# A sum of weights made by an accumulating transfer within SBUF, in place of an addition on VectorE

## The chip, the cores and the metric

The kernel runs on one core of one Trainium2 chip. The metric is device time in microseconds (us) of one execution; a lower time is better. Before the change it took 2020.15 us, the median of 3 runs (2019.51 to 2020.68).

## The reference

A decoder trunk of two layers, in float32, on 512 tokens with 16 learned tokens ahead (T = 528), width 1024, hidden width 2816. Cut to what matters here:

```python
def swiglu(x, w_in, w_out):
    gate, up = jnp.split(x @ w_in, 2, axis=-1)
    return (jax.nn.silu(gate) * up) @ w_out

for i in range(2):                                   # h: (528, 1024)
    h = h + 0.5 * swiglu(rmsnorm(h, norm_ffn1[i]), ffn1_w_in[i], ffn1_w_out[i])
    h = h + mixer_i(rmsnorm(h, norm_mix[i]))         # retention in layer 0, gated linear attention in layer 1
    h = h + 0.5 * swiglu(rmsnorm(h, norm_ffn2[i]), ffn2_w_in[i], ffn2_w_out[i])
return rmsnorm(h, final_norm)[:, 16:]
```

The change touches the last product of swiglu, `(...) @ w_out`, in each of the four feed-forward networks.

## The kernel before

**Names of the networks.** f1/0 and f2/0 are the networks ahead of and behind the mixer of layer 0, f1/1 and f2/1 those of layer 1. The first three are *feeding*: as their last columns of x are finished, the kernel already scales and splits them for the next block (`feed`). f2/1 is the last.

**Precision.** A float32 operand is split into a high part and a low part, and each product is three matmuls (`mm3`, L488 to L490): high by high, high by low, low by high. A weight tile of 128 rows by 512 (or 384) columns comes to SBUF as `raw`. ScalarE makes its high part by a cast (`whi`, L188) and VectorE its low part by a subtraction (`wlo`, L189). This pair of instructions stands once for each weight tile, some 1200 times in a run, and TensorE multiplies by the results four steps later at most (`AHEAD = 4`).

**Units.** Most products are done in *units*: two blocks of output rows and two halves of the tokens, by a scheme with seven products in place of eight. Its seven weight operands are a11, a12, a22 as loaded, s1 = a21 + a11, s3 = a21 + a22, s2 = s1 + a11 and s4 = a12 + s2 (signs are hidden in the data). Their order in a unit is a11, s1, s2, a12, s4, s3, a22 (`UNIT`). The first unit of a feeding network's last group has the order a11, s1, a12, s2, s4, s3, a22 (`PARTED`): its first three products are each done in two parts, so that work can begin before the last hidden rows are there. A unit's results are X (one bank) and Q, Z (two banks) in PSUM. The last product, a22, is held over and done inside the next unit. Each bank is emptied by ScalarE copies (L727, L729, L734: `szf<-X` and the like) or by VectorE additions before TensorE writes it again.

**How the sums are made.** For each unit, SP (SyncE's DMA queue) loads a11 and a22 into the two halves of a `pair` tile (L149), and GpSimd (POOL) then issues one transfer from HBM that adds a21 to both halves (L155; in some units two transfers, L153). The pair's halves then hold s3 and s1. a11, a12 and a22 are also loaded by SP as `raw` tiles (L158). After the split of a11, VectorE adds s1 to the raw tile of a11 (L195): that tile now holds s2. After the split of a12, VectorE adds s2 to the raw tile of a12 (L197): that tile now holds s4. There are 7 raw tiles and 3 pair tiles. GpSimd's queue holds little else than these transfers in the network stages; a transfer for a later unit waits there until its pair tile is free and its first halves are loaded.

**Out groups.** The 22 blocks of hidden rows are consumed in groups: 8, 6 and 8 in a feeding network, 6, 6, 6 and 4 in the last one. Group index 2 is the last group in a feeding network (8 blocks, four products of 128 columns of k: weight tiles of 128x512) and the third of four in f2/1 (6 blocks: 128x384). A group has four units, d = 0, 2, 4, 6, each for two of the eight blocks of x. Its units are called `unit_o`; the in-products are units too (`unit_g`, `unit_u`), with two units per pair of hidden blocks.

**Where results go.** The names carry the unit: Xf10u is the X bank of a u unit of f1/0, Xf10o that of an o unit. L1035 (`su<-Xf10u,su`) empties X of the last u unit on VectorE. L1069 and L1070 add an o unit's first row to x, L1076 and L1077 the second (`x<-szf,x`, then `x<-Xf10o,x`, which frees X); L1081 adds the a22 product. L576 and L592 scale, square and split x for the next block.

**What sets the order.** The program is written as one stream; a scheduler puts each engine's instructions into a row by priorities, and each engine runs its row strictly in order. An instruction that waits holds all that stands behind it on its engine. `_split` issues one operand's cast, subtraction and sums, and is called up to four steps ahead of the product that uses it.

Of the kernel before, what the change touches and what calls it, by code (L numbers as in the profile page):

```python
# [14 lines left out]
ALU = mybir.AluOpType  # L15
# [53 lines left out]
class Weights:  # L69
# [92 lines left out]
    def _split(self, upto):  # L162
        V = self.nc.vector
        while self.split < min(upto, len(self.plan)):
            i = self.split
            home = next(((pool, there) for pool, n, there in self.homes if len(there) < n), None)
            if not home:
                break
            home[1].add(i)
            _, c, q, n, order = self.plan[i]  # L170
            self._load()
            if order:

                late = order[0] == "s1"
                s2 = self.tiles[c][:, 1] if late else self.tiles[c, "a11"]
                raw = {"s1": self.tiles[c][:, 1], "s3": self.tiles[c][:, 0], "s2": s2,
                       "s4": self.tiles[c, "a12"]}.get(q)
            if not order or raw is None:
                raw = self.tiles[c, q]
            hi = home[0].tile([P, PW], F32R, tag="hi", name=f"whi{i}")  # L180
            lo = home[0].tile([P, PW], F32R, tag="lo", name=f"wlo{i}")
            with ExitStack() as order_:
                if self.behind and i < self.FRONT:
                    for ins in self.behind:
                        order_.enter_context(self.tc.issue_after(ins.ins))
                if self.after:
                    order_.enter_context(self.tc.issue_after(self.after.ins))
                act = self.nc.scalar.copy(hi[:, :n], raw)  # L188
                dve = V.tensor_sub(lo[:, :n], raw, hi[:, :n].bitcast(F32))  # L189
                self.newest = act, dve  # L190
            self.parts[i] = (hi, lo)
            self.split += 1
            if order:
                if q == ("s1" if late else "a11"):
                    V.tensor_add(s2, self.tiles[c][:, 1], self.tiles[c, "a11"])  # L195
                elif q == "a12":
                    V.tensor_add(raw, raw, s2)  # L197
                self.over["pair"] += q == "s3"
                self.over["raw"] += q in self.OVER[2 if order == self.PARTED else late]
            else:  # L200
                self.over["raw"] += 1
            self._load()
# [2146 lines left out]
```

## Time and profile before

One execution was profiled: its own time was 2020.17 us, its span 2018.4 us.

| | value |
|---|---|
| median of the runs | 2020.15 us (2019.51 to 2020.68) |
| profiled execution | 2020.17 us, span 2018.4 us, granted TensorE clock 0.999 |
| TensorE (PE) busy | 1998.6 us, 99% of the span, 16576 matmuls |
| VectorE (DVE) busy | 1793.7 us, 89%, 3302 instructions |
| ScalarE (ACT) busy | 1190.6 us, 59%, 2427 instructions |
| GpSimd (POOL) busy | 209.8 us, 10%, 181 instructions |
| casts of weights (L188, raw and pair) | 715.3 us on ACT, 1197 instructions |
| subtractions of weights (L189, raw and pair) | 792.1 us on DVE, 1197 instructions |
| sums on DVE, L195 and L197 | 97.2 us and 97.5 us, 146 of each in the usual form |
| moved by DMA | 318.87 MB, mean 158 GB/s |

How it is read: a share is busy time over the span. The page has, after the busy times, the span in 40 slices, the DMA queues (a queue's share is of 16 DMA engines over the span), the chain of work that ended last, and the groups of instructions by line, engine, operation and tiles. A row of single instructions gives the start, the duration, the engine, the line, the operation, the output and inputs, and in square brackets the idle time before it with what ended it. A line "DMA to landing" below a transfer gives the time from its issue to the moment when the last of its data has arrived. A row of waits gives the waiting engine, tile and line, what it waited for, and us in all, times, and the longest.

### The profile page before, as it was taken

Reading aid. Unit: us, or ns where it says so; the run is one execution under the profiler, and the core shown is the slowest. Engines: PE = TensorE matmul, PEld = TensorE weight load, DVE = VectorE, ACT = ScalarE, POOL = GpSimd, SP = SyncE. Lnnn points to the kernel's source line nnn. Section 1 sums busy time; section 2 is a strip of 40 time slices with the busy share of each in tenths; the row PEclk is TensorE's granted clock in tenths of the full one; section 3 lists DMA queues with packets and bytes.
Section 4 is the critical chain, followed back from the end, with each engine's and each line's share of the span. In section 5 each row is a group of like instructions: output and inputs, shape, how many; then the busy total and the mean of one; then the engine's idle time right before and its main releaser. Section 6 shows DMA issues by size and latency. Waiting matters only on the chain.

```text
span 2018.4 us, 43487 instructions
## 1 busy us (share of the span) xinstructions
PE 1998.6 (99%) x16576; PEld 1964.3 (97%) x16576; DVE 1793.7 (89%) x3302; ACT 1190.6 (59%) x2427; POOL 209.8 (10%) x181
## 2 busy tenths in 40 slices
PE   9999999999999999999999999999999999999998
PEld 9999999999999999999999999999999989999998
DVE  8999999978787889989999998999897868999896
ACT  5756566555555465656666665666745544666664
POOL 1011111010101000111111011111001000211110
PEclk9999999999999999999999999999999999999999
DMA  7586877364545432776875477777525441687772
GB/s 228 138 208 168 205 194 188 101 163 121 157 132 147 132 116 74 181 202 161 213 186 163 128 189 187 180 199 181 183 69 126 105 137 65 159 208 182 185 191 69
DMA packets 176113, 318.87 MB, mean 158 GB/s; under 512 B 17568, under 2 KB 40736, under 8 KB 175904
## 3 DMA queue, kind: packets, MB, share of 16 engines
q1 hardware_dynamic: 133856, 237.04, 35.8%
q0 software_dynamic: 40896, 75.51, 23.4%
q10 hardware_dynamic: 1152, 3.55, 0.6%
q8 instruction: 130, 2.13, 0.4%
q14 instruction: 79, 0.65, 0.1%
HBM read 311.76 MB, written 4.26 MB: 157 GB/s over the span
## 4 chain that ended last, share of the span: by engine, by line
PE 83%; DVE 12%; ACT 2%; issue 2%; DMA 1%; POOL 0%; POOLq 0%; DVEq 0%; ACTq 0%
DVE wlo L189 4%; PE po_r L488 1%; PE po_r L489 1%; PE po_r L490 1%; PE lv L1866 1%; ACT whi L188 1%; DVE hf L521 1%; PE Xf21o L488 1%; PE Xf21o L490 1%; PE Xf21o L489 1%; PE Xf20u L488 1%; PE Xf11u L488 1%; PE Xf20u L490 1%; PE Xf11u L490 1%; PE Xf11u L489 1%
## 5 line engine op out<-in xcount | busy, mean ns | idle before, releaser
L188 ACT CAST whi<-raw 128x512 fp32r<-128x512 f32 (+1 forms) x893 | 531.9, 606 | 424.6 <-DVE raw L197 145.9
L189 DVE TENSOR_TENSOR wlo<-raw,whi 128x512 fp32r<-128x512 f32 (+1 forms) x893 | 590.3, 669 | 104.6 <-ACT whi L188 91.4
L188 ACT CAST whi<-pair 128x512 fp32r<-128x512 f32 (+1 forms) x304 | 183.4, 604 | 75.1 <-DVE pair L195 12.4
L189 DVE TENSOR_TENSOR wlo<-pair,whi 128x512 fp32r<-128x512 f32 (+1 forms) x304 | 201.8, 665 | 11.7 <-ACT whi L188 10.6
L155 POOL DMA_DIRECT2D pair<-in_f_in x73 | 89.0, 1220 | 704.6 <-DVE wlo L189 348.0
L197 DVE TENSOR_TENSOR raw<-raw,raw 128x512 f32<-128x512 f32 (+1 forms) x146 | 97.5, 668 | 3.6
L195 DVE TENSOR_TENSOR raw<-pair,raw 128x512 f32<-128x512 f32 (+1 forms) x146 | 97.2, 666 | 3.4 <-DMA pair<-in_f_in 0.8
L155 POOL DMA_DIRECT2D pair<-in_f_out x44 | 53.5, 1216 | 358.3 <-DVE wlo L189 122.8
L488 PE MATMUL po_r<-ogh,whi 128*128 128x264 f32 x256 | 71.7, 280 | 0.1
L489 PE MATMUL po_r<-ogl,whi 128*128 128x264 f32 x256 | 71.5, 279 | 0.0
L490 PE MATMUL po_r<-ogh,wlo 128*128 128x264 f32 x256 | 71.2, 278 | 0.0
L155 POOL DMA_DIRECT2D pair<-in_ret_in x20 | 24.4, 1222 | 308.6 <-DVE wlo L189 156.3
L999 ACT ACTIVATE gf<-gf 128x528 f32<-128x528 f32 (+1 forms) x36 | 23.2, 644 | 50.4 <-DVE gf L998 50.3
L488 PE MATMUL Xf11o<-hf,whi 128*128 128x264 f32 x176 | 49.5, 281 | 1.4 <-ACT szf L734 0.4
L488 PE MATMUL Xf20o<-hf,whi 128*128 128x264 f32 x176 | 49.5, 281 | 1.4 <-DVE x L1077 0.6
L488 PE MATMUL Xf10o<-hf,whi 128*128 128x264 f32 x176 | 49.5, 281 | 1.0 <-ACT szf L734 0.4
L489 PE MATMUL Xf11o<-hf,whi 128*128 128x264 f32 x176 | 49.1, 279 | 0.0
L489 PE MATMUL Xf20o<-hf,whi 128*128 128x264 f32 x176 | 49.1, 279 | 0.0
L489 PE MATMUL Xf10o<-hf,whi 128*128 128x264 f32 x176 | 49.1, 279 | 0.0
L488 PEld LDWEIGHTS po_r<-ogh,whi 128*128 128x128 f32 x256 | 48.0, 188 | 0.9 <-ACT k L521 0.3
L490 PE MATMUL Xf20o<-hf,wlo 128*128 128x264 f32 x176 | 48.9, 279 | 0.0
L490 PE MATMUL Xf10o<-hf,wlo 128*128 128x264 f32 x176 | 48.9, 279 | 0.0
(1183 smaller groups left out, 8598.8 us busy)
## 6 DMA issues: line engine op xcount, KB each, us to landing
raw<-in_f_in SPq DMA_DIRECT2D x277, 256.0 KB, 3.7
pair<-in_f_in SPq DMA_DIRECT2D x150, 256.0 KB, 5.0
pair<-in_f_in POOLq DMA_DIRECT2D x73, 512.0 KB, 7.4
raw<-in_f_out SPq DMA_DIRECT2D x80, 256.0 KB, 3.3
raw<-in_ret_in SPq DMA_DIRECT2D x76, 256.0 KB, 3.0
raw<-in_f_out SPq DMA_DIRECT2D x72, 192.0 KB, 3.0
pair<-in_f_out SPq DMA_DIRECT2D x48, 256.0 KB, 4.9
pair<-in_f_out POOLq DMA_DIRECT2D x24, 512.0 KB, 6.1
```

The lines of the kernel that those rows point to most:

```text
L155: nc.gpsimd.dma_start(t, aps[2].unsqueeze(1).broadcast_to([P, 2, n]), accum_op=ALU.add)
L188: act = self.nc.scalar.copy(hi[:, :n], raw)
L189: dve = V.tensor_sub(lo[:, :n], raw, hi[:, :n].bitcast(F32))
L195: V.tensor_add(s2, self.tiles[c][:, 1], self.tiles[c, "a11"])
L197: V.tensor_add(raw, raw, s2)
L488: nc.tensor.matmul(ps, lhsT=lh, rhs=rh, start=start, stop=False, **kw)
L489: nc.tensor.matmul(ps, lhsT=lh, rhs=rl, start=False, stop=False, **kw)
L490: return nc.tensor.matmul(ps, lhsT=ll, rhs=rh, start=False, stop=stop, **kw)
L521: return S.copy(hi, src), V.tensor_sub(lo, src, hi.bitcast(F32))
L999: S.activation(o, o, AF.Silu, scale=-1.0)
L1866: nc.tensor.matmul(ps[:, j, J * P:J * P + n], lhsT=Kt[:, j, J * P:(J + 1) * P], rhs=q, start=(J == 0), stop=(J == 3), skip_group_check=True)
```

## The change

In the units with key ("o", 2), that is in group index 2 of every network, s2 is no longer made by VectorE's addition. GpSimd issues a transfer instead that reads s1 from the pair tile in SBUF and accumulates it onto the raw tile of a11 in SBUF. `late` is true only in the order `FIRST`, which begins with s1 and which no out unit has; so the first unit of each feeding network's last group (order `PARTED`) has the transfer too, and so have the four units of the last network's third group. That makes 16 units: 12 with tiles of 128x512 and 4 with 128x384. VectorE has 16 additions less, GpSimd 16 transfers more. The added lines shift the later line numbers by 3: L197 becomes L200, L1035 becomes L1038, L1077 becomes L1080; the new transfer is L196.

```diff
-            _, c, q, n, order = self.plan[i]
+            key, c, q, n, order = self.plan[i]
...
             if order:
                 if q == ("s1" if late else "a11"):
-                    V.tensor_add(s2, self.tiles[c][:, 1], self.tiles[c, "a11"])
+                    if key[2:4] == ("o", 2) and not late:
+                        self.nc.gpsimd.dma_start(s2, self.tiles[c][:, 1], accum_op=ALU.add)
+                    else:
+                        V.tensor_add(s2, self.tiles[c][:, 1], self.tiles[c, "a11"])
                 elif q == "a12":
                     V.tensor_add(raw, raw, s2)
```

The order of GpSimd's row in the last group of f1/0. The pair tiles of its four units are pair_4010, pair_4148, pair_4276 and pair_4455, their a11 tiles raw_4065, raw_4215, raw_4316 and raw_4505; pair_4794 and pair_4924 belong to the retention block behind. Before:

```order
L155 DMA pair_4148<-in_f_out 128x2x512
L155 DMA pair_4276<-in_f_out 128x2x512
L155 DMA pair_4455<-in_f_out 128x2x512
L155 DMA pair_4794<-in_ret_in 128x2x512
L155 DMA pair_4924<-in_ret_in 128x2x512
```

After:

```order
L155 DMA pair_4148<-in_f_out 128x2x512
L155 DMA pair_4276<-in_f_out 128x2x512
L196 DMA raw_4065<-pair_4010 128x512
L155 DMA pair_4455<-in_f_out 128x2x512
L196 DMA raw_4215<-pair_4148 128x512
L196 DMA raw_4316<-pair_4276 128x512
L155 DMA pair_4794<-in_ret_in 128x2x512
L196 DMA raw_4505<-pair_4455 128x512
L155 DMA pair_4924<-in_ret_in 128x2x512
```

The first unit's transfer stands behind the third unit's pair transfer, the second unit's behind the fourth's; the third unit's stands right behind the second's, and the fourth's behind the first pair transfer of the next block.

VectorE's row at the first unit of that group, where raw_4065 is a11 and raw_4110 is a12. Before:

```order
L189 TENSOR_TENSOR wlo_4332<-raw_4065,whi_4331 128x512
L195 TENSOR_TENSOR raw_4065<-pair_4010,raw_4065 128x512
L189 TENSOR_TENSOR wlo_4349<-pair_4010,whi_4348 128x512
L189 TENSOR_TENSOR wlo_4368<-raw_4110,whi_4367 128x512
L197 TENSOR_TENSOR raw_4110<-raw_4110,raw_4065 128x512
L189 TENSOR_TENSOR wlo_4398<-raw_4065,whi_4397 128x512
L1035 TENSOR_TENSOR su_4352<-Xf10u_4237,su_4239 128x264
```

After:

```order
L189 TENSOR_TENSOR wlo_4332<-raw_4065,whi_4331 128x512
L189 TENSOR_TENSOR wlo_4349<-pair_4010,whi_4348 128x512
L189 TENSOR_TENSOR wlo_4368<-raw_4110,whi_4367 128x512
L200 TENSOR_TENSOR raw_4110<-raw_4110,raw_4065 128x512
L189 TENSOR_TENSOR wlo_4398<-raw_4065,whi_4397 128x512
L1038 TENSOR_TENSOR su_4352<-Xf10u_4237,su_4239 128x264
```

The addition is gone from ahead of the split of s1; what reads raw_4065 as s2, the addition into raw_4110 and the split into wlo_4398, keeps its place ahead of the emptying of Xf10u.

VectorE's row at the second unit, where pair_4148 holds s1, raw_4215 is a11 and raw_4257 is a12; raw_4129 is the first unit's a22, and x_80 and x_79 are blocks of x. Before:

```order
L1076 SCALAR_TENSOR_TENSOR x_80<-szf_4414,x_80 128x264
L195 TENSOR_TENSOR raw_4215<-pair_4148,raw_4215 128x512
L189 TENSOR_TENSOR wlo_4485<-pair_4148,whi_4484 128x512
L189 TENSOR_TENSOR wlo_4502<-raw_4129,whi_4501 128x512
L1069 SCALAR_TENSOR_TENSOR x_79<-szf_4414,x_79 128x528
L189 TENSOR_TENSOR wlo_4531<-raw_4215,whi_4530 128x512
L1070 SCALAR_TENSOR_TENSOR x_79<-QZf10o_4413,x_79 128x528
L189 TENSOR_TENSOR wlo_4552<-raw_4257,whi_4551 128x512
L1077 SCALAR_TENSOR_TENSOR x_80<-Xf10o_4412,x_80 128x264
```

After:

```order
L1079 SCALAR_TENSOR_TENSOR x_80<-szf_4414,x_80 128x264
L189 TENSOR_TENSOR wlo_4485<-pair_4148,whi_4484 128x512
L189 TENSOR_TENSOR wlo_4502<-raw_4129,whi_4501 128x512
L1072 SCALAR_TENSOR_TENSOR x_79<-szf_4414,x_79 128x528
L189 TENSOR_TENSOR wlo_4531<-raw_4215,whi_4530 128x512
L1073 SCALAR_TENSOR_TENSOR x_79<-QZf10o_4413,x_79 128x528
L189 TENSOR_TENSOR wlo_4552<-raw_4257,whi_4551 128x512
L1080 SCALAR_TENSOR_TENSOR x_80<-Xf10o_4412,x_80 128x264
```

The split of s2 (wlo_4531), which now waits for GpSimd's transfer, keeps its place ahead of the emptying of Xf10o (now L1080).

## The prediction

> **What bounds the kernel now.** I read the page's first lines, then the engines' busy time by stage (stages found by the line numbers of the out units), then who waits for whom there, then the rows of single units.
>
> ```profile
> span 2018.4 us, 43487 instructions
> PE 1998.6 (99%) x16576; PEld 1964.3 (97%) x16576; DVE 1793.7 (89%) x3302; ACT 1190.6 (59%) x2427; POOL 209.8 (10%) x181
> ```
>
> TensorE (PE) has 20 us of idle time in the whole span. The stages in which the change acts, by the same view cut to four stretches (columns: length, then busy us and count of PE, weight load, VectorE, ScalarE, GpSimd; granted clock; DMA share; GB/s):
>
> ```profile
> 290.00:348.00 58.00, 56.86 (x478) 56.03 (x477) 56.02 (x105) 40.66 (x85) 7.29 (x6) 1.00 0.70 178
> 1032.00:1094.00 62.00, 60.79 (x512) 59.98 (x511) 59.97 (x112) 43.00 (x89) 7.31 (x6) 1.00 0.72 184
> 1368.00:1425.00 57.00, 55.90 (x474) 55.31 (x473) 54.97 (x104) 38.47 (x83) 6.20 (x6) 1.00 0.75 193
> 1918.00:1958.00 40.00, 40.00 (x345) 40.00 (x344) 37.46 (x74) 25.07 (x57) 4.83 (x4) 1.00 0.78 198
> ```
>
> The first three are the feeding out groups of f1/0, f2/0 and f1/1, the fourth the third out group of f2/1. PE and VectorE (DVE) are both nearly full, 98% and 97% in the first. PE's waits in that first stretch, and its longest wait of the whole run:
>
> ```profile
> PE Xf10o L488 <- ACT szf L734: 0.4, 1, 0.4
> PE Xf10o L488 <- ACT szf L729: 0.3, 1, 0.3
> PE Xf10o L488 <- DVE x L1077: 0.3, 1, 0.3
> ...
> PE idle L413 <- DVE rc L459: 1.1, 1, 1.1
> ```
>
> So DVE, though full, costs PE 1.0 us per feeding group, some 3 us over the three. More than that cannot be gained by relieving it there: a bound of 3.0 us, below the 4 us (0.2%) that a measurement of this kernel can tell from no change.
>
> **What is removed.** 16 additions: 12 of the form in this row, 4 of 384 columns.
>
> ```profile
> L195 DVE TENSOR_TENSOR raw<-pair,raw 128x512 f32<-128x512 f32 x4 | 2.7, 687 | 0.0
> ```
>
> Queued instructions of this size start 0.6 us apart, so DVE gets back 12 x 0.6 + 4 x 0.47 = 9.1 us, of which PE can see at most the 3.0 us above. I book 0, because the waits below use DVE's time up first.
>
> **What is added.** 16 transfers on GpSimd's queue. No row has one from SBUF to SBUF; the nearest rows are accumulating transfers from HBM on the same queue (issues: KB each, median us from issue to landing; then min/median/max of the unbroadcast ones of line 153, issued in twos):
>
> ```profile
> q0 software_dynamic: 40896, 75.51, 23.4%
> ...
> pair<-in_f_out POOLq DMA_DIRECT2D x20, 384.0 KB, 5.6
> ...
> DMA to landing us min/median/max: 3.7/4.8/8.3
> ```
>
> The queue used 23.4% of 2018.4 us for 75.51 MB, so 256 KB (0.262 MB) takes 1.64 us of data time and 192 KB 1.23. A 512 KB transfer that lands in 6.1 (row below) would then land in 6.1 - 1.64 = 4.5 at half the size, and the 384 KB one in 5.6 - 1.23 = 4.4 at half. I take 4.5 and 4.4 for a transfer alone, near the 4.8 of the row, with 3.7 and some 6.0 (4.5 plus one more data time) as ends. Behind another transfer of the queue I take that one's landing plus 1.64. The Trainium skill (DMA: Bandwidth & Descriptors, section Anatomy of one DMA) gives 2.0 us plus bytes/436e3, an estimate of 2.6 us alone for 256 KB; by it the sum below would be about 37 us in place of 60. The rows here are slower than that even when nothing else of the queue is in flight, so the rows decide.
>
> After a wait that another engine ends, GpSimd starts its transfer about 0.7 us late (SP's loads land 0.7 to 0.9 before the pair rows start).
>
> ```profile
> 1739.82 0.87 POOL L153 DMA_DIRECT2D pair<-in_f_out  x1 [0.73 <-DMA pair<-in_f_out]
> ```
>
> **Term A, the first unit of a feeding group.** The new order puts its transfer behind the pair transfer of the third unit, and DVE's add of line 197 (s4 = a12 + s2, now line 200) waits for it. Behind that add stands L1035, which frees the bank X for PE's last product of the u unit before.
>
> ```profile
> 298.31 1.21 POOL L155 DMA_DIRECT2D pair<-in_f_out  x1 [6.62 <-DVE wlo L189]
> DMA to landing us min/median/max: 6.1/6.1/6.1
> 298.84 0.69 DVE L197 TENSOR_TENSOR raw<-raw,raw 128x512 f32<-128x512 f32 x1
> 300.33 0.43 DVE L1035 TENSOR_TENSOR su<-Xf10u,su 128x264 f32<-128x264 f32 x1
> 301.53 0.28 PE L488 MATMUL Xf10u<-thf,whi 128*128 128x264 f32 x1
> ```
>
> The pair lands at 304.4, s2 at 306.05. L197 starts 7.2 us late; L1035 then ends near 307.8 (0.67 + 0.60 + 0.43 later) and PE's product slips from 301.53 by 6.3. DVE has no gap in the hidden rows that follow (only 0.2 us up to L1035), and the group's last k step needs them, so PE ends the unit some 7.0 late. In the other two groups the pair lands later against the add:
>
> ```profile
> 1045.43 1.22 POOL L155 DMA_DIRECT2D pair<-in_f_out  x1 [7.25 <-DMA pair<-in_f_out]
> DMA to landing us min/median/max: 6.8/6.8/6.8
> 1044.76 0.69 DVE L197 TENSOR_TENSOR raw<-raw,raw 128x512 f32<-128x512 f32 x1
> ...
> 1380.58 1.22 POOL L155 DMA_DIRECT2D pair<-in_f_out  x1 [6.92 <-DVE wlo L189]
> DMA to landing us min/median/max: 7.1/7.1/7.1
> 1380.10 0.69 DVE L197 TENSOR_TENSOR raw<-raw,raw 128x512 f32<-128x512 f32 x1
> ```
>
> 1045.43 + 6.8 + 1.64 - 1044.76 - 0.2 = 8.9, and 1380.58 + 7.1 + 1.64 - 1380.10 - 0.2 = 9.0. A = 7.0 + 8.9 + 9.0 = 24.9 us.
>
> **Term B, the second unit.** Its transfer stands behind the fourth unit's pair transfer, which itself needs the first unit's s3 split and SP's load, so all of this moves with A and can be read in the old clock. Behind the late split stand L1070, one more split and L1077, which frees X for the a22 product held over from the unit before.
>
> ```profile
> 308.80 1.22 POOL L155 DMA_DIRECT2D pair<-in_f_out  x1 [9.27 <-DVE x L1076]
> DMA to landing us min/median/max: 5.9/5.9/5.9
> 312.95 0.42 DVE L1077 SCALAR_TENSOR_TENSOR x<-Xf10o,x 128x264 f32<-128x264 f32 x1
> 314.90 0.28 PE L488 MATMUL Xf10o<-hf,whi 128*128 128x264 f32 x1
> ```
>
> The pair lands at 314.7, s2 at 316.3. ScalarE casts it (the split follows the cast's start by 0.66), DVE splits from 317.0, and L1077 ends at 317.0 + 0.6 + 0.6 + 0.6 + 0.42 = 319.25 where PE wants 314.90: 4.35 us. ScalarE is held too, with the evacuation L729 behind it, but that comes out inside the same wait.
>
> **Terms C and D, the third and fourth units.** Here GpSimd waits for the split of a11 and nothing stands ahead.
>
> ```profile
> 317.36 0.68 DVE L189 TENSOR_TENSOR wlo<-raw,whi 128x512 fp32r<-128x512 f32 x1
> 324.70 0.28 PE L488 MATMUL Xf10o<-hf,whi 128*128 128x264 f32 x1
> ...
> 328.82 0.69 DVE L189 TENSOR_TENSOR wlo<-raw,whi 128x512 fp32r<-128x512 f32 x1
> 334.50 0.28 PE L488 MATMUL Xf10o<-hf,whi 128*128 128x264 f32 x1
> ```
>
> C: a11 is split at 318.04; plus 0.7, 4.5 and 0.66 the s2 split starts at 323.9; a12's split (0.6), two L576 (0.8) and L1077 follow, so X is free at 326.3, 1.6 late. DVE enters 1.3 later against PE than before (5.9 lost in B, PE lost 4.35, some of it caught up): 2.9. D: 329.5 + 5.86 = 335.4, and with 0.6, 0.6, 0.68 and 0.43 X is free at 337.7, 3.2 late, less 0.8 that DVE gains on PE after C: 2.4. B + C + D = 9.65 per group, 28.9 for three.
>
> **Term E, the last network's third group.** The same pattern with 384 columns; its first unit's cast now stands behind the two ScalarE copies it could have held, so I book nothing for that one. For the second:
>
> ```profile
> 1927.59 0.56 DVE L189 TENSOR_TENSOR wlo<-raw,whi 128x384 fp32r<-128x384 f32 x1 [0.38 <-ACT whi L188]
> ...
> 1934.72 0.28 PE L488 MATMUL Xf21o<-hf,whi 128*128 128x256 f32 x1
> ```
>
> 1928.15 + 0.7 + 4.4 + 0.55 = 1933.8, and seven DVE instructions up to L1077's end take 3.5: 1937.3, 2.6 late. The third and fourth meet the same wait with DVE already late by 0.8 more than PE, and gain an eviction now ahead of the split: 1.9 each. E = 6.4.
>
> Sum: 24.9 + 28.9 + 6.4 = 60.2 us slower. The profiled execution took 2020.17 us (span 2018.4), 0.02 over the median 2020.15, so the forecast is 2020.2 + 60.2 = 2080.4.
>
> **Bounds.** If each transfer lands in 3.7 and does not queue behind a pair, A falls to 4.2 + 5.4 + 5.2 = 14.8, B to 1.75, C and D to 1.6 each, E to 4.3: 34 us, 2054. If single transfers take 6.0 and queued ones land 3.2 after the pair (1.6 more), A gains 4.8, B 4.8, C and D 9.0, E 4.8: 83.6 us, 2104.
>
> **Rivals.** First, only A is paid. The splits run up to four steps ahead of PE, a step is 12 products of 0.117 us (1.4 us), and the order has moved evictions about; if that slack takes B to E up, 24.9 us remain: 2045. Against it: L1077 ends 1.5 us before PE's product in B's rows and stands behind the waiting split.
>
> Second, PE's clock. In the stages above it was granted 1.00, with no PE wait above 1.1 us. A is three stalls of 6 to 9 us and B three of 4. If the clock fell to half after each, for as long as the stall, PE would lose half of 24.9 + 13.1, 19 us: 2099. The Trainium skill (TensorE: Matmul & The Clock Gate, Part 1) says that about 3.4 us of idling halves the clock and about 3.4 us of work restores it; by its figure six stalls would cost some 10 us. No run here shows a long stall.
>
> Third, on the other side, not slower: the transfer is hidden and only DVE's relief is left, 2017 to 2020. It takes over from the point where s2 lands within about 2.9 us of its issue in C. But in A the queue is not free until 299.52 and the add needs s2 at 298.84, so even a landing in 2 us leaves PE late by over 2 us per group; A would have to vanish with it.
>
> Fourth, that the change does other than it says is partly so: the order shows 16 transfers, not the nine that its words suggest. Nine alone would be B to D, 28.9 us, 2049.
>
> **Numbers.** Forecast 2080 (2054 to 2104): 0.62. Only A: 0.16. Half clock: 0.13. Not slower: 0.05 (0.04 same, 0.01 faster, as relief is bounded at 3.0 us). Above 2104: 0.04. The range reaches from 2035, the first rival with A at its lower bound of 14.8, to 2104. Slower by over 0.2%: 0.95.
>
> **What would show it.** PE's list of waits: entries of 6 to 9 us for Xf10u, Xf20u and Xf11u on L1038 (the old L1035), entries of 2 to 4 us for the o units on L1080 (the old L1077). DVE's and ScalarE's: waits for raw<-pair transfers in L200, L189 and L188. New rows of 16 POOL transfers of some 0.9 us, landing in 4 to 5 alone. A granted clock under 1.00 there would speak for the second rival. I am wrong if the transfers land in about 2 us, or if PE keeps under 2 us of waits per group.

## The result, and the profile after

The changed kernel takes 2077.58 us, the median of 5 runs (2074.76 to 2080.07), against 2019.51 us before on the same chip: a ratio of 1.0286, with a 95% interval of 1.0271 to 1.0301. It is 58.1 us slower by the medians. The profiled execution took 2075.67 us. Its first lines:

```profile
span 2073.9 us, 43534 instructions
PE 2015.8 (97%) x16576; PEld 1979.4 (95%) x16576; DVE 1786.1 (86%) x3286; ACT 1190.4 (57%) x2427; POOL 224.1 (11%) x197
```

The span grew by 55.5 us. TensorE's idle time grew from 19.8 us (2018.4 - 1998.6) to 58.1, that is by 38.3, and its busy time by 17.2 for the same 16576 matmuls. So 38 us are waits and 17 us are matmuls that took longer, by the profile's account of busy time. VectorE is 7.6 us less busy.

Where it was lost shows in the first matmuls of the blocks behind f1/0 with the retention, behind f2/0, behind f1/1 and at the end. Before:

```profile
759.99 0.36 PE L488 MATMUL pf20g<-nhf,whi 128*128 128x264 f32 x1
1095.08 0.37 PE L488 MATMUL pf11g<-nhf,whi 128*128 128x264 f32 x1
1431.32 0.37 PE L1754 MATMUL pg_gz<-uhgla,whi 128*128 128x264 f32 x1
2010.45 0.61 PE L1259 MATMUL st_fb<-ones,endh 128*128 128x1 f32 x4
```

After:

```profile
776.48 0.37 PE L491 MATMUL pf20g<-nhf,whi 128*128 128x264 f32 x1
1127.99 0.37 PE L491 MATMUL pf11g<-nhf,whi 128*128 128x264 f32 x1
1480.34 0.37 PE L1757 MATMUL pg_gz<-uhgla,whi 128*128 128x264 f32 x1
2065.93 0.61 PE L1262 MATMUL st_fb<-ones,endh 128*128 128x1 f32 x4
```

The differences are 16.5, 32.9, 49.0 and 55.5 us: 16.5, 16.4 and 16.1 us for the three feeding groups, 6.5 for the last network. TensorE's waits (us in all, times, longest) in the changed kernel:

```profile
PE Xf20u L491 <- DVE su L1038: 7.0, 1, 7.0
PE Xf11u L491 <- DVE su L1038: 6.8, 1, 6.8
PE Xf10u L491 <- DVE su L1038: 5.8, 1, 5.8
PE Xf11o L491 <- DVE x L1080: 4.0, 3, 3.3
PE Xf20o L491 <- DVE x L1080: 3.8, 3, 2.5
PE Xf10o L491 <- DVE x L1080: 3.8, 2, 2.6
PE Xf21o L491 <- DVE x L1080: 3.0, 2, 1.9
PE Xf10o L491 <- ACT szf L732: 2.5, 1, 2.5
PE Xf20o L491 <- ACT szf L732: 2.1, 1, 2.1
...
PE Xf21o L491 <- ACT su L737: 1.4, 1, 1.4
```

They are where the prediction put them: one long wait per feeding group at the evacuation of X (19.6 us), and shorter ones in the o units. Not all end with VectorE: the last three end with a ScalarE copy (ACT). The new transfers, their landing, and who waited for them:

```profile
L196 POOL DMA_DIRECT2D raw<-pair x16: 861/921/1437, 298.8 to 1995.3; - x16
...
  ACT whi L188: 65.1, 16
  DVE raw L200: 23.1, 3
...
DMA to landing us min/median/max: 3.3/5.0/6.7
```

All 16 were waited for. The first unit of f1/0, GpSimd, VectorE and TensorE, in three answers of the timeline:

```profile
298.04 1.21 POOL L155 DMA_DIRECT2D pair<-in_f_out  x1 [6.59 <-DMA raw<-in_f_out]
298.77 1.44 POOL L196 DMA_DIRECT2D raw<-pair  x1
...
305.53 0.69 DVE L200 TENSOR_TENSOR raw<-raw,raw 128x512 f32<-128x512 f32 x1 [6.99 <-DMA raw<-pair]
...
307.28 0.59 PE L491 MATMUL Xf10u<-thf,whi 128*128 128x264 f32 x1 [5.85 <-DVE su L1038]
307.66 0.42 PE L492 MATMUL Xf10u<-tlf,whi 128*128 128x264 f32 x1
307.88 0.42 PE L493 MATMUL Xf10u<-thf,wlo 128*128 128x264 f32 x1
```

The add of line 200 waits 6.99 us on VectorE, line 1038 stands behind it, and TensorE waits 5.85 us for X. The matmuls behind the wait start 0.22 us apart (307.66, 307.88), where they were 0.117 apart before it. By stretches (length, busy us and count of PE, weight load, VectorE, ScalarE, GpSimd; granted clock; DMA share; GB/s):

```profile
301.20:307.30 6.10, 0.25 (x3) 0.05 (x2) 1.77 (x4) 1.58 (x3) 0.00 (x0) 0.84 0.60 109
307.30:312.00 4.70, 4.70 (x21) 4.70 (x22) 4.36 (x10) 2.02 (x6) 0.00 (x0) 0.50 0.70 196
```

The granted clock is 0.50 for the 4.7 us behind the wait. The rows of all groups show seven such stretches of 2.4 to 5.3 us, 122 matmul steps in all; 122 x (0.22 - 0.117) = 12.5 us lost, of the 17.2 above; the other 4.7 were not placed. The kernel before has no such stretch in these groups. Below, "half pace" means such a stretch.

### The profile page after: what moved, and what is told of

Same layout as the page of the kernel before. It is cut to its first block, busy times and chain, and to the rows that moved or that the text cites. A ratio compares the mean times of both kernels' runs of the same rounds, so it can differ in the third digit from the quotient of the medians.

```text
span 2073.9 us, 43534 instructions
## 1 busy us (share of the span) xinstructions
PE 2015.8 (97%) x16576; PEld 1979.4 (95%) x16576; DVE 1786.1 (86%) x3286; ACT 1190.4 (57%) x2427; POOL 224.1 (11%) x197
## 4 chain that ended last, share of the span: by engine, by line
PE 80%; DVE 9%; DMA 6%; ACT 2%; issue 2%; POOL 0%; SPq 0%; ACTq 0%; POOLq 0%; DVEq 0%
DMA raw<-pair 4%; DVE wlo L189 3%; PE po_r L491 2%; PE po_r L492 1%; PE po_r L493 1%; ACT whi L188 1%; PE lv L1869 1%; DVE hf L524 1%; DMA raw<-in_f_out 1%; PE Xf11o L491 1%; PE Xf21u L491 1%; PE Xf20o L491 1%; PE Xf20u L491 1%; PE Xf21u L492 1%; PE Xf21u L493 1%
## 5 line engine op out<-in xcount | busy, mean ns | idle before, releaser
L188 ACT CAST whi<-pair 128x512 fp32r<-128x512 f32 (+1 forms) x304 | 183.2, 603 | 78.1 <-DVE pair L198 12.4
L200 DVE TENSOR_TENSOR raw<-raw,raw 128x512 f32<-128x512 f32 (+1 forms) x146 | 97.4, 667 | 26.5 <-DMA raw<-pair 23.1
L198 DVE TENSOR_TENSOR raw<-pair,raw 128x512 f32<-128x512 f32 (+1 forms) x130 | 86.6, 667 | 3.4 <-DMA pair<-in_f_in 0.8
L493 PE MATMUL Xf11o<-hf,wlo 128*128 128x264 f32 x176 | 50.0, 284 | 0.0
```

The source lines that it names most:

```text
L493: return nc.tensor.matmul(ps, lhsT=ll, rhs=rh, start=False, stop=stop, **kw)
```

## The experiments

Each was timed beside the kernel before on one chip, in two lots (before: 2020.63 and 2021.38 us).

**Only the second to fourth units.** The condition of the change becomes

```diff
-if key[2:4] == ("o", 2) and not late:
+if key[2:4] == ("o", 2) and key[:2] != ("f2", 1) and key[4]:
```

> The transfer is made only in the second to fourth units of the three feeding networks (9 units); the first units and the last network keep VectorE's addition. Theory (each unit waits for its own transfer): with no first stall, TensorE comes to the second unit on time and meets B in full, so B + C + D of the prediction, 9.65 us per group, and a little of the clock, 0 to 1.4 us per group: 2048 to 2053, taken as 2050. Rival 1 (what is lost there in the changed kernel is what these units cost, some 6.5 us of waits and 1.3 of clock per group): 2043. Rival 2 (only the first units cost): 2020 to 2022.

Measured: 2050.13 us, ratio 1.0144 (1.013 to 1.0158), 29.5 us. TensorE's waits:

```profile
PE Xf20o L491 <- DVE x L1080: 5.3, 2, 5.0
PE Xf10o L491 <- DVE x L1080: 5.1, 1, 5.1
PE Xf11o L491 <- DVE x L1080: 4.9, 3, 4.4
```

Without a first stall the second unit waits 5.1, 5.0 and 4.4 us; term B had 4.35. In the changed kernel that wait is 1.24 us in f1/0, 1.08 in f2/0 and 0.41 in f1/1. So a first stall hides most of the second. The sum of the theory came true, but not unit by unit: behind the long second wait the third unit waits 0.2 us at most, where term C had 2.9, and the fourth 1.8 to 2.2. The listed waits come to some 22 us, and half pace (72 steps) adds 7.4, where at most 4.2 were expected.

**Only the first units.** The same line with `not key[4]` in place of `key[4]`.

> The transfer is made only in the first unit of the three feeding networks (3 units). Theory: three TensorE waits of 5.8 to 7.0 us (19.6 in all) and 2.1 to 2.5 us of half pace after each (7.0): 26.6 us, 2046. By the prediction's term A alone, without a clock loss: 24.9 us, 2045; the two are told apart by the waits and the matmul spacing, not by the time. Rival (VectorE, held up by one stall, is late for the units behind as well): 2050 or more.

Measured: 2049.15 us, ratio 1.0137 (1.0123 to 1.0151), 28.5 us.

```profile
PE Xf20u L491 <- DVE su L1038: 7.7, 1, 7.7
PE Xf11u L491 <- DVE su L1038: 7.1, 1, 7.1
PE Xf10u L491 <- DVE su L1038: 5.6, 1, 5.6
```

The waits come to 20.4 us, and half pace behind the three takes 6.4 (62 steps). That is 26.8; the time is some 2 us above it and 1 below the rival's 2050, but the o units show no new waits that would bear the rival out.

**Only the last network.** The condition becomes `key[2:4] == ("o", 2) and key[:2] == ("f2", 1)`.

> The transfer is made only in the four units of the last network's third group. Theory: the last stage loses what it lost in the changed kernel, 6.5 us (term E was 6.4): 2026. Rival (the last group is late only because of what went before it): 2020.

Measured: 2028.54 us, ratio 1.0036 (1.0022 to 1.0049), 7.9 us. The last group's loss is its own; it is 1.4 us more than the 6.5 of the changed kernel. The three parts together come to 29.5 + 28.5 + 7.9 = 65.9 us, 8 more than the whole change cost. Stalls hide one another in part: the second units' waits come to 14.5 us in the run of nine and to 2.7 in the changed kernel, while the third units' go the other way, from 0.2 to 8.3. That is 3.7 of the 8 us; less half pace (106 steps in the three groups, 134 in the two runs) is another 2.9.

**No sum at all.**

```diff
-self.nc.gpsimd.dma_start(s2, self.tiles[c][:, 1], accum_op=ALU.add)
+pass
```

> In the 16 units s2 is not formed at all (a11 is used in its place), neither on VectorE nor by a transfer: VectorE's relief alone. Theory (term booked at 0, bound 3.0 us): 2017 to 2020, taken as 2019. Rival (VectorE, 97% busy in these stages, is a second bound there, and its 9.1 us come back): 2011 to 2016.

Measured: 2022.38 us, ratio 1.0005 (0.9996 to 1.0014): no change. The median lies above the theory's range, which allowed for a small gain. The span of its profile is 2017.4 us, 1.0 less than before's:

```profile
span 2017.4 us, 43479 instructions
PE 1998.5 (99%) x16576; PEld 1964.8 (97%) x16576; DVE 1784.9 (88%) x3286; ACT 1192.8 (59%) x2427; POOL 209.5 (10%) x181
```

VectorE is 8.8 us less busy, and TensorE is idle for 18.9 us in place of 19.8. By the interval a faster way of making these 16 sums could gain 0.04% at most in this order of the program.

**Sum and transfer.** Starting from the kernel before, with `key` unpacked as in the change:

```diff
 elif q == "a12":
     V.tensor_add(raw, raw, s2)
+elif q == "s1" and key[2:4] == ("o", 2):
+    self.nc.gpsimd.dma_start(raw, self.tiles[c][:, 0], accum_op=ALU.add)
```

> VectorE makes s2 as before, and the 16 units issue a transfer of the same size on the same queue as well, which adds one half of the pair tile onto the other after the last reading of that half (a sum that nobody uses): the queue and the traffic as changed, without anyone who waits for the result. Theory (what costs is VectorE and ScalarE waiting for the landing): 2019 to 2022. Rival (what costs is the queue: 16 more transfers hold back the pair transfers behind them, or take the 16 DMA engines from SP's loads): 2030 or more.

Measured: 2030.77 us (four runs, 2025.21 to 2035.58), ratio 1.0055 (1.0037 to 1.0073). The median falls just into the rival's range, but 9.4 us remain of the 58.1: waiting for the result is most of the cost, and the 16 transfers cost something even when nobody reads their result.

The profiled execution took 2025.21 us. In its out groups TensorE has no wait longer than before's and no half pace. What is late is the next block: GpSimd's second transfer for the retention, before and here, ScalarE's cast at its entry, before and here, then a wait of SP over the whole run that before does not have, and TensorE's clock at that entry:

```profile
333.09 1.21 POOL L155 DMA_DIRECT2D pair<-in_ret_in  x1 [9.39 <-DVE x L1070]
...
342.77 1.31 ACT L188 CAST whi<-raw 128x512 fp32r<-128x512 f32 x2 [0.46 <-DMA raw<-in_ret_in]
```

```profile
341.14 1.22 POOL L155 DMA_DIRECT2D pair<-in_ret_in  x1 [5.30 <-DMA pair<-in_ret_in]
...
345.06 1.28 ACT L188 CAST whi<-raw 128x512 fp32r<-128x512 f32 x2 [2.70 <-DMA raw<-in_ret_in]
...
SPq L149 <- DMA pair<-pair: 58.3, 14, 7.8
...
351.50:356.00 4.50, 4.50 (x22) 4.50 (x22) 3.57 (x8) 0.62 (x1) 1.93 (x2) 0.50 1.08 338
```

The second pair transfer is issued 8.1 us later, and ScalarE waits 2.70 us for weights in place of 0.46; TensorE then runs 4.4 us at half pace at the entry of that block. It begins the retention's first product 0.1 us late and its second one 4.8 us late, nearly all that this trace lost. The rows show a way to this delay that the rival does not name. The added transfer works on the pair tile, and SP, before it loads the next first halves into that tile, waits 14 times for such a transfer to land, 58.3 us in all. SP's later loads stand behind that wait. The 9.4 us are therefore not shown to be the cost of GpSimd's queue: the held tile and the queue were not tried apart. In the changed kernel the same transfer holds a raw tile in place of the pair's half; what that costs there is not shown either. The other three executions, 2030.6 to 2035.6 us, have no trace; where their further 5 to 10 us lie stays open.

**The addition on GpSimd.**

```diff
-self.nc.gpsimd.dma_start(s2, self.tiles[c][:, 1], accum_op=ALU.add)
+self.nc.gpsimd.tensor_add(s2, self.tiles[c][:, 1], self.tiles[c, "a11"])
```

> In the 16 units GpSimd adds s2 itself, by an addition in SBUF in the same place of its row, in place of the transfer. No row has such an addition on GpSimd at this size; between VectorE's 0.69 us and four times that. Theory (the place in the row costs only in the first units, where the pair transfer ahead is not issued before 299.3 while the add of line 200 wants s2 at 298.8; the others have 2.9 us): 1 to 3 us in each of three groups, 2020 to 2028, taken as 2024. Rival (GpSimd's additions slow VectorE or come as late as the transfers): 2040 or more. Second rival (all hidden, with VectorE's relief): 2017 to 2020.

Measured: 2039.98 us, ratio 1.0092 (1.0076 to 1.0108). The theory missed by 16 us, and the time is at the lower end of the rival's. TensorE waits 1.1 to 2.1 us at the first units, as the theory had it, and 1.1 us at a time in the o units, where it had nothing. A reason shows in the rows of GpSimd's addition and VectorE's split in the same stretch:

```profile
310.44 1.76 POOL L196 TENSOR_TENSOR raw<-pair,raw 128x512 f32<-128x512 f32 x1
...
310.80 1.95 DVE L189 TENSOR_TENSOR wlo<-pair,whi 128x512 fp32r<-128x512 f32 x1
```

The split takes 0.69 us elsewhere and 1.95 here: it ends 0.55 us after GpSimd's addition. Beside 13 of the 16 additions one VectorE instruction is lengthened in this way, to between 1.07 and 2.46 us; beside the other three, those of the first units, VectorE was waiting. The Trainium skill (GPSIMD Engine Reference, section 1, Specifications) says that GpSimd shares its ways into SBUF with VectorE and that the two contend when a VectorE instruction has two SBUF inputs. This pair of rows agrees, though an instruction with two inputs that began 0.02 us after the addition (310.46, line 1079) kept its usual 0.42 us. So the sums cost VectorE no less when GpSimd makes them: it is 1797.0 us busy here, 1793.7 before and 1784.9 with the sums left out.

**The transfer ahead of the pair.** The first unit's transfer is put in the queue ahead of the third unit's pair transfer, in the three feeding networks:

```diff
+key = self.plan[first][0]
+if kind == "pair" and key[2:5] == ("o", 2, 4) and key[:2] != ("f2", 1) and self.split <= first - 13:
+    break
...
+with self.tc.issue_after(self.s2.ins) if turned else ExitStack():
     nc.gpsimd.dma_start(t, aps[2].unsqueeze(1).broadcast_to([P, 2, n]), accum_op=ALU.add)
...
-self.nc.gpsimd.dma_start(s2, self.tiles[c][:, 1], accum_op=ALU.add)
+self.s2 = self.nc.gpsimd.dma_start(s2, self.tiles[c][:, 1], accum_op=ALU.add)
```

> As changed, but the first unit's transfer is issued ahead of the third unit's pair transfer in the three feeding networks. Theory (the first stall is mostly the queue: landing alone in 4.5 after an issue at 297.3, so the add of line 200 starts near 302 in place of 305.5): first stalls of 2 to 3.5 us in place of 5.8 to 7.0, and the second units' wait grows towards the 4.4 to 5.1 us that they have without a first stall: 2062 to 2069, taken as 2065. Rival (the place in the queue does not matter, the landing of a transfer within SBUF is long in that stage anyway): 2075 to 2080.

Measured: 2064.57 us, ratio 1.0207 (1.0181 to 1.0233). Line 205 is the add that was line 200, line 1043 the evacuation, line 1085 that of the o units:

```profile
297.84 0.91 POOL L201 DMA_DIRECT2D raw<-pair  x1 [5.33 <-DVE wlo L194]
...
302.08 0.69 DVE L205 TENSOR_TENSOR raw<-raw,raw 128x512 f32<-128x512 f32 x1 [2.60 <-DMA raw<-pair]
...
PE Xf20u L496 <- DVE su L1043: 2.4, 1, 2.4
PE Xf11u L496 <- DVE su L1043: 2.1, 1, 2.1
PE Xf10u L496 <- DVE su L1043: 1.5, 1, 1.5
PE Xf10o L496 <- DVE x L1085: 4.7, 2, 3.5
```

The same transfer lands 4.2 us after its issue instead of 6.7, the first stall falls to 1.5 to 2.4 us, and the second unit's wait grows to 3.5 in f1/0 and to 3.4 and 3.2 in the other two groups. The theory held in time (2065 expected) and mechanism; the first stalls came out at or below its low end.

**A late evacuation, without any transfer.** In the kernel before:

```diff
+if last:
+    m = {"f10": 6, "f20": 12, "f11": 24}[me]
+    V.tensor_reduce(o, c.unsqueeze(2).broadcast_to([P, HT, m]), axis=mybir.AxisListType.X, op=ALU.max)
 V.tensor_add(o, c, s)
```

> The kernel before, with no transfer; in the last u unit of the three feeding networks one added VectorE instruction (a maximum over 6, 12 and 24 repeats of the same X, overwritten at once) holds up line 1035's evacuation by some 2.3, 3.9 and 7.2 us. Theory (TensorE's pace falls because of its own waits, whatever causes them): TensorE waits of about 1.6, 3.2 and 6.5 us; none or little half pace after the first, 2.0 to 2.5 us lost to it after the third, the second in between; 2033 to 2037. Rival (the half pace belongs to the transfers): matmuls 0.117 us apart right after each wait, 2031 or less.

Measured: 2040.85 us, one run. The added instruction took 1.81, 3.46 and 6.76 us. The order of the rows changed with it: in f1/0 14 matmuls of the o unit (1.6 us) stand ahead of X's product. So the first two delays gave no wait at X, and only the third did, of 3.19 us in place of the expected 6.5:

```profile
1401.81 0.39 PE L488 MATMUL Xf11u<-thf,whi 128*128 128x264 f32 x1 [3.19 <-DVE su L1038]
...
1401.80:1405.50 3.70, 3.69 (x17) 3.69 (x18) 2.80 (x8) 1.87 (x5) 0.00 (x0) 0.54 0.01 4
```

The sizes were missed, and the time lies above the theory's range. The question was answered: behind a wait that VectorE made, with 1% DMA share, the clock is 0.54 for 3.7 us. So half pace needs no transfer within SBUF.

This stall accounts for little of the 20 us. The first matmul into QZf11u, ahead of the third delay, already starts 12.4 us late (1139.12 against 1126.74), with few waits listed: VectorE, 97% busy in these groups before, has 12.0 us more to do, and TensorE's matmuls there start further apart. Nine us less of VectorE's work gained nothing, and 12 us more cost 20; how the 20 divide between the added work and the changed order is not shown.

## Why the prediction was right, point by point

The time was forecast at 2080.4 and is 2077.58; 60.2 us were forecast and 58.1 measured. The mechanism (VectorE and ScalarE wait for the landing, and TensorE for the banks behind them) and its places were right. That the sum came so near is partly luck: 60.2 us were booked as waits, where TensorE's idle time grew by 38.3, and the clock was booked at nothing, where matmuls took 17.2 longer.

- **What bounds it, and the relief of 0.** Right, and shown: leaving the sums out altogether gives 1.0005. But the bound of 3.0 us was read too high: of the three waits listed for the first group two end with ScalarE (lines 734 and 729), and only 0.3 us ends with VectorE.
- **The price of a transfer.** Forecast 4.5 us alone and a pair's landing plus 1.64 behind one. Measured alone, 4.0 to 5.4 for 256 KB and 3.3 to 5.3 for 192 KB; behind the pair, in f1/0 298.77 + 6.7 - (298.04 + 6.1) = 1.33, and 1.2 to 1.9 in all six. The formula of the Trainium skill (DMA: Bandwidth & Descriptors, Anatomy of one DMA), whose estimate was 2.6 us alone, is below the shortest landing of all 16.
- **Term A**, 24.9 us: the waits are 19.6, 5.3 too high. In all three groups the prediction took VectorE's lateness, less 0.2, for TensorE's; for f1/0 it had the product 6.3 late and raised that to 7.0. VectorE waits 6.99, 8.11 and 7.97 us at line 200 and TensorE 5.85, 6.97 and 6.83: 1.1 us less each time, the lead of the evacuation on the product. With the half pace behind the stalls (20, 24 and 24 steps, 7.0 us), A cost 26.6.
- **Term B**, 13.05 us: 2.7 measured. The step that failed is "all of this moves with A and can be read in the old clock". The pair transfer that B waits behind started 5.2 us later than before in f1/0 (314.00 against 308.80), while TensorE was 5.85 us late by its wait and 2.06 more by its pace. So the transfer was 2.7 us less late than TensorE, and the wait shrank. The first experiment shows the 4.4 to 5.1 us that B costs when TensorE is not held up ahead of it.
- **Terms C and D**, 15.9 us: the waits of this size above are 2.6, 2.5, 3.3 at line 1080 and 2.5, 2.1 at line 732, with about 1 in f1/1; 14 in all. Nearly right in size, with 4.0 us of half pace on top. But the fourth unit's wait ends with ScalarE's copy (line 732), where the prediction had VectorE's line 1080; and in the run of nine, where the second unit's wait was long, the third unit's was not there, so its size depends on what comes before.
- **Term E**, 6.4 us: 6.5 in the changed kernel, 7.9 alone. Right in the sum, by two errors: the waits are 4.4 us, 2.0 too high in the prediction, and half pace (16 steps) makes up most of the rest.
- **The rival of the clock**, given 0.13: its mechanism is real (clock 0.50, 12.5 us of half pace), and the time stayed in the forecast's range because the waits were smaller than booked. That TensorE at half pace arrives later at the next wait, and so waits less there, fits the rows of f1/0 under term B, but was not tried apart. The prediction treated the two as separate. By the figure of the Trainium skill (TensorE: Matmul & The Clock Gate, Part 1) six stalls were put at some 10 us, near the 12.5. That is partly chance: the six were those of A and B, and half pace came behind A's three, three of C and D and one of E, none of B.
- **"Only A is paid"** is refuted by the nine units' 29.5 us, **"not slower"** by every run that has the transfer.
- **What was not booked:** what the transfers cost beside their readers. Sixteen whose result nobody reads still cost 0.37 to 0.73%, with SP waiting for the tiles that they hold.

## What to carry to other kernels

A transfer in place of an addition of 0.7 us puts a landing of 3 to 7 us into a chain of dependences; it must be issued that much ahead of its reader, and what an in-order engine holds behind the reader is what is paid. Before moving work off a full engine, leave it out once and time that: here it gained nothing, though VectorE was 97% busy. Stalls are not added one by one: here a first stall let the next transfer catch up, and the single parts came to 8 us more than the whole.

## What the runs showed of the hardware

The clock fell behind some waits and not behind others, and their length did not decide. In the changed kernel a wait of 1.87 us was followed by half pace and one of 2.59 was not:

```profile
337.22 0.36 PE L491 MATMUL Xf10o<-hf,whi 128*128 128x264 f32 x1 [2.59 <-DVE x L1080]
1994.09 0.38 PE L491 MATMUL Xf21o<-hf,whi 128*128 128x256 f32 x1 [1.87 <-DVE x L1080]
...
337.20:341.00 3.80, 3.78 (x32) 3.80 (x33) 3.46 (x8) 3.04 (x7) 0.00 (x0) 1.00 0.84 176
1994.10:1998.00 3.90, 3.90 (x21) 3.90 (x22) 2.60 (x6) 1.62 (x5) 0.92 (x1) 0.60 0.94 270
```

The Trainium skill (TensorE: Matmul & The Clock Gate, Part 1) tells of a free-running window of about 3.4 us in which TensorE's activity is judged. That the length alone does not decide agrees with such a window. That a wait of 1.87 us is enough does not agree with that part's table of the two states, which has the slow clock after at least one idle window. The run with sum and transfer goes further: its half pace from 351.6 on stands behind waits of 0.49 us at most, in a stretch (344.00 to 351.50) in which TensorE was busy for 6.29 of 7.50 us. What the window counts was not tried.
